# Whole-row gathers for the last four iterations of each stage of a PEER trunk

## The chip, the cores and the metric

The kernel runs on one core of a Trainium2 chip. The metric is the device time in microseconds, lower is better. Times are given as medians of several executions; a profile is one further execution, with a time of its own.

The engines that matter here are TensorE (PE, matrix products into PSUM), VectorE (DVE), ScalarE (ACT), GpSimd (POOL, which issues the gathers), and the core's 16 DMA engines.

## The reference

A decoder trunk of four layers works on 256 tokens of width 1024. Each layer has a token mixer (HGRN2, FoX attention, Mamba-2, HGRN2), and behind it a PEER block. PEER is what the change touches. For each token and each of 8 heads it scores two sets of 128 sub-keys, takes the 16 best of the 16 x 16 sums, and so gets 16 expert numbers out of 16384 with softmax gates. Then

```python
u = jnp.take(u_tab, idx, axis=0)
v = jnp.take(v_tab, idx, axis=0)
act = jax.nn.gelu(jnp.einsum('md,mhkd->mhk', xb, u), approximate=False) * gates
return jnp.einsum('mhk,mhkd->md', act, v)
```

So each token reads 128 rows of `u_tab` and up to 128 rows of `v_tab`, 4 KB each in float32, for every layer. Where the GELU is exactly zero, the V row adds nothing and needs no reading. The arguments of the GELU are spread wide by the inputs' scale, so that this happens.

## The kernel before

**Stages and iterations.** There are eight stages: four layers by two blocks of 128 tokens. Stage s runs 64 iterations, one for each pair (head, q), and each iteration handles two experts for all 128 tokens. Its 256 rows are laid out as two halves: half g holds tokens 64 g to 64 g + 63, with the first expert of the pair on partitions 0 to 63 and the second on partitions 64 to 127. In this text k is the number of an iteration within its stage (`i % 64` in the code), from 0 to 63; numbers from 64 up belong to the next stage.

**Buffers.** U and V lie side by side in one table `uv`, a row of 8 KB holding [U|V]. Eight buffers `GB` (L197), each 128 x 2048 floats (1.05 MB), take the gathered rows: iteration i uses `GB[2i % 8]` for half 0 and `GB[(2i+1) % 8]` for half 1. A pair's buffers are thus used again four iterations later.

**Gathers.** POOL issues all of them, in the order of the program. `fetch` (L1268) gathers U or whole rows; for half 1 always whole [U|V] rows, for half 0 the U half only, except in the first eight iterations of the program (`WHOLE`). In this text these are W(k) for half 1, and U(k) for half 0. `fetches(n)` (L1277) runs at the head of each iteration and sends U and W up to three iterations ahead. `second` (L1283) gathers the V rows of half 0, V(k), once the GELU of half 0 is known: two DVE instructions (L1296, L1297) add a large number to the row's index where the GELU is zero, and the gather's bounds check then leaves the row out. In the last two iterations of a stage (`early`, L1265) V(k) is gathered one iteration sooner, from the plain index (L1292, L1293), with no row left out.

**One iteration.** `fetches`, `dot` of half 0 and of half 1 (L1301: DVE multiplies U by the tokens' activations XR and sums, ACT takes the GELU), `second`, then `spread` (L1315): ACT multiplies by the gates and makes a 128 x 64 matrix of them for each half (`dg`), and PE multiplies these with the V rows (L1335) and adds into two PSUM banks. Half 1 is summed in its own iteration. Half 0 is summed `LAG` = 2 iterations later, since V(k) comes in late; in the last two iterations of a stage and in the first eight of the program it is summed in its own iteration. Behind this stand three steps of routing on DVE (which experts the next heads take) and a slot of side work: the mixer and the query projection for stage s + 1, whose weights come by SP's DMA queue.

**End of a stage.** After iteration 62 all remaining side work is done, and `repeated()` (L1246, L1463) puts 64 small products on PE's queue: they lay out the next stage's activations. ACT and DVE copy them from PSUM to XR (L1442 and L1453 on ACT, L1454 on DVE) during iteration 63, each after the `dot` that reads the old XR. The `dot` of the next stage's first iteration stands behind these copies. Up to three pairs of the next stage have been gathered ahead by then.

The engines take their instructions in program order. A gather into a buffer waits (on POOL, in order) until those who read the buffer before are done; everything that POOL has to issue behind it waits too.

Of the kernel before, what the change touches and what calls it, by code (L numbers as in the profile page):

```python
# [10 lines left out]
F32 = mybir.dt.float32  # L11
# [5 lines left out]
OP = mybir.AluOpType  # L17
AX = mybir.AxisListType

P = 128  # L20
T = 256
D = 1024
DC = D // P
DEPTH = 4
# [4 lines left out]
NQ = TOPK // 2  # L29
NGB = 8  # L30
NRAW = 3
LAG = 2
WHOLE = 8
FAR = 1048576.0
STAGES = 2 * DEPTH

# [132 lines left out]
def trunk(ctx: ExitStack, tc: tile.TileContext, d: dict, out: bass.AP):  # L169
    nc = tc.nc  # L170
# [3 lines left out]
    wk2 = ctx.enter_context(tc.tile_pool(name="wk2", bufs=2))  # L174
# [22 lines left out]
    GB = [at_["gb"][:, i * 2 * D:(i + 1) * 2 * D] for i in range(NGB)]  # L197
# [12 lines left out]
    vec = Vector()  # L210
# [79 lines left out]
    for l in range(DEPTH):  # L290
        nm = ("hg%d" % (l // 3), "fox", "ssm", "hg%d" % (l // 3))[l]
        n = UNITS[KIND[l] if KIND[l] != "ssd" else "ssm"]
# [8 lines left out]
    for u in range(28, len(stream)):  # L301
        t, l, i, where = places[u]
# [864 lines left out]
    def route(s, hh):  # L1167

        l = s // 2
        sv = wk2.tile([P, 2, TOPK], F32, name="sv")  # L1170
        si = wk2.tile([P, 2, TOPK], U32, name="si", bufs=1)
        sf = wk2.tile([P, 2, TOPK], F32, name="sf", bufs=1)
        ts = wk2.tile([P, TOPK], F32, name="ts")
        ti = wk2.tile([P, TOPK], U32, name="ti", bufs=1)
        ab = wk2.tile([P, 2, TOPK], U32, name="ab", bufs=1)
        af = wk2.tile([P, 2, TOPK], F32, name="af", bufs=1)
        cs = wk2.tile([P, TOPK * TOPK], F32, name="cs", bufs=1)
        eq = cs.bitcast(BF16).rearrange("p (c k j) -> p c k j", c=2, k=TOPK)
        cs = cs.rearrange("p (a b) -> p a b", a=TOPK)
        ix = wk2.tile([P, 2, NQ], I32, name="ix", bufs=4)  # L1180
        gs = wk2.tile([P, 2, 2, NQ], F32, name="gs", bufs=4)
        gt = wk2.tile([P, 4], F32, name="gt")
        ig = wk2.tile([P, 2, TOPK], F32, name="ig")
        yield from top16([(sv[:, c], si[:, c], SS[:, hh, c]) for c in range(2)])
        vec.tensor_copy(sf, si)
        tm(cs, sv[:, 0].unsqueeze(2).to_broadcast([P, TOPK, TOPK]),
           sv[:, 1][:, None, :].to_broadcast([P, TOPK, TOPK]), op=OP.add)
        yield
        yield from top16([(ts, ti, cs.rearrange("p a b -> p (a b)"))])
        vec.tensor_scalar(ab[:, 0], ti, 4, None, op0=OP.logical_shift_right)  # L1190
        vec.tensor_scalar(ab[:, 1], ti, 15, None, op0=OP.bitwise_and)
        vec.tensor_copy(af, ab)
        m, z, r = (gt[:, i:i + 1] for i in range(3))
        vec.tensor_scalar(m, ts[:, 0:1], -1.0, None, op0=OP.mult)
        act(ig[:, 1], ts, AF.Exp, bias=m, accum_out=z)
        yield
        eqv = eq.rearrange("p c k j -> p (c k) j")
        tm(eqv, C("iota")[:, None, :].to_broadcast([P, 2 * TOPK, TOPK]),
           af.rearrange("p c k -> p (c k)").unsqueeze(2).to_broadcast([P, 2 * TOPK, TOPK]), op=OP.is_equal)
        yield  # L1200
        tm(eq, eq, sf.unsqueeze(2).to_broadcast([P, 2, TOPK, TOPK]), op=OP.mult)
        yield
        vec.tensor_reduce(af.rearrange("p c k -> p (c k)"), eqv, axis=AX.X, op=OP.add)
        vec.tensor_scalar(sf[:, 0], af[:, 0], float(P), float(l * P * P), op0=OP.mult, op1=OP.add)
        tm(ig[:, 0], sf[:, 0], af[:, 1], op=OP.add)
        yield
        igv = ig.rearrange("p c (q j) -> p c q j", j=2)
        places = [(slice(j * 64, j * 64 + 64), g, slice(g * 64, g * 64 + 64), j) for j in range(2) for g in range(2)]

        def scaled():  # L1210
            vec.reciprocal(r, z)
            vec.tensor_scalar(ig[:, 1], ig[:, 1], r, None, op0=OP.mult)

        if (s, hh) == (0, 0):

            for o, g, i, j in places:
                vec.tensor_copy(ix[o, g], igv[i, 0, :, j])
            scaled()
            for o, g, i, j in places:
                vec.tensor_copy(gs[o, g, 1], igv[i, 1, :, j])  # L1220
        else:
            scaled()
            yield
            for o, g, i, j in places:
                vec.tensor_copy(gs[o, g], igv[i, :, :, j])
            vec.tensor_copy(ix, gs[:, :, 0])
            vec.tensor_scalar(ix[:, 0], gs[:, 0, 0], 2.0, None, op0=OP.mult)
            vec.tensor_scalar(gs[:, 0, 0], gs[:, 0, 0], 2.0, 1.0, op0=OP.mult, op1=OP.add)
        got[s, hh] = ix, gs

    heads = [(s, hh) for s in range(STAGES) for hh in range(8)]
# [30 lines left out]

    parts = d["uv"].rearrange("r (k n) -> (r k) n", k=2)

    def early(i):  # L1265
        return i % 64 >= 64 - LAG

    def fetch(n):  # L1268
        i, g = divmod(n, 2)
        s, hh, q = pairs[i]  # L1270
        to, src = GB[n % NGB], d["uv"]
        if not g and i >= WHOLE:
            to, src = to[:, 0:D], parts
        nc.gpsimd.indirect_dma_start(to, None, src,  # L1274
                                     bass.IndirectOffsetOnAxis(ap=got[s, hh][0][:, g, q:q + 1], axis=0))

    def fetches(n):  # L1277

        while sent[0] < 2 * len(pairs) and sent[0] < 2 * n + NGB and pairs[sent[0] // 2][:2] in got:
            fetch(sent[0])  # L1280
            sent[0] += 1

    def second(i):  # L1283

        if i < WHOLE or i >= len(pairs):
            return
        s, hh, q = pairs[i]
        iv = wk2.tile([P, 1], I32, name="iv", bufs=4)
        row = got[s, hh][1][:, 0, 0, q:q + 1]
        to = GB[2 * i % NGB][:, D:2 * D]  # L1290
        if early(i):
            nc.vector.tensor_copy(iv, row)  # L1292
            nc.gpsimd.indirect_dma_start(to, None, parts, bass.IndirectOffsetOnAxis(ap=iv, axis=0))  # L1293
        else:
            far = wk2.tile([P, 1], F32, name="far", bufs=2)
            nc.vector.tensor_scalar(far, acts[i][:, 1, 0:1], 0.0, FAR, op0=OP.is_equal, op1=OP.mult)  # L1296
            nc.vector.tensor_tensor(iv, far, row, op=OP.add)  # L1297
            nc.gpsimd.indirect_dma_start(to, None, parts, bass.IndirectOffsetOnAxis(ap=iv, axis=0),  # L1298
                                         bounds_check=2 * DEPTH * P * P - 1, oob_is_err=False)

    def dot(i, g):  # L1301
        if g == 0:
# [12 lines left out]
    def spread(i):  # L1315
        s, hh, q = pairs[i]
        a = acts.pop(i)
        for g in range(2):
            act(a[:, 2, g:g + 1], a[:, 1, g:g + 1], AF.Copy, scale=got[s, hh][1][:, g, 1, q:q + 1])
        for g in range(2):  # L1320
            diags[i, g] = wk2.tile([P, 64], F32, name="dg%d" % g, bufs=4 - g)
            act(diags[i, g], m64, AF.Copy, scale=a[:, 2, g:g + 1])
        if hh == 0 and q == 0:
            accs[s] = [accp.tile([P, 512], F32, name="acc") for _ in range(2)]
        if i == len(pairs) - 1:
            warm(3, bank(), cst)
        sums = [(i, 1)]
        if i < WHOLE or early(i):
            sums.append((i, 0))
        if (i - LAG, 0) in diags:  # L1330
            sums.insert(0, (i - LAG, 0))
        for e in range(2):
            for j, g in sums:
                v = GB[(2 * j + g) % NGB][:, D + e * 512:D + (e + 1) * 512]
                nc.tensor.matmul(accs[s][e][g * 64:g * 64 + 64], diags[j, g], v, start=j % 64 == 0,  # L1335
                                 stop=j % 64 == 63)
        for k in sums:
            diags.pop(k)
# [71 lines left out]
    for s in range(STAGES):  # L1410
# [23 lines left out]
        for i in range(64 * s, 64 * s + 64):  # L1434
            new, end = i % 64 == 0 and s > 0, i % 64 == 63 and s + 1 < STAGES
            fetches(i)
            if early(i + 1):
                second(i + 1)
            dot(i, 0)
            if end:  # L1440
                for o, b in x[:2]:
                    nc.scalar.copy(o, b)  # L1442
            elif new:

                products_(True)
                others()
            dot(i, 1)
            if not early(i):
                second(i)
            spread(i)  # L1450
            if end:
                (_, b), (o, c) = x[2:]
                nc.scalar.copy(x[2][0], b)  # L1453
                vec.tensor_copy(o, c)  # L1454
            route_steps(3, i // 8 + 3)
            others()
            products_()
            if i % 64 == 62 and s + 1 < STAGES:
                while not state["done"]:
                    others()  # L1460
                    products_(True)
                others()
                x = repeated()  # L1463
            if table[0] is not AF.Gelu:
                act(spare, eps, AF.Gelu)
# [20 lines left out]
```

## Time and profile before

| | us |
|---|---|
| three timed executions | 3212.19, 3215.95, 3218.97 |
| median | 3215.95 |
| the profiled execution: its own time | 3209.99 |
| the profiled execution: span of the core | 3208.2 |

| engine | busy us | share of the span |
|---|---|---|
| PE | 2506.6 | 78% |
| DVE | 2232.1 | 70% |
| POOL | 1799.3 | 56% |
| ACT | 1383.7 | 43% |

DMA moved 1271.08 MB at a mean of 396 GB/s, 1041.70 MB of them by the gathers (the queue named software_dynamic). In the rows that follow, `arena<-in_uv,ix` is a U or W gather, `arena<-in_uv,iv` a V gather; L1335 is the sum into the accumulators, L1274 the issue of U and W, L1298 and L1293 the issue of V, L207 any of the DVE helper's instructions. A row of the timeline has the start, the duration, the engine, the line and the operation, and in square brackets how long the engine was idle before it and who ended that wait. A row of the windows view has a stretch of time, its length, busy time and number of instructions of PE, PE's weight loads, DVE, ACT and POOL, then the granted PE clock (1 is full), the busy share of the DMA engines and what they moved in GB/s. The rows do not tell the iteration: it is found by counting the gathers and the sums back from the 64 products at a stage's end.

### The profile page before, as it was taken

Reading aid. Unit: us, or ns where it says so; the run is one execution under the profiler, and the core shown is the slowest. Engines: PE = TensorE matmul, PEld = TensorE weight load, DVE = VectorE, ACT = ScalarE, POOL = GpSimd, SP = SyncE. Lnnn points to the kernel's source line nnn. Section 1 sums busy time; section 2 is a strip of 40 time slices with the busy share of each in tenths; the row PEclk is TensorE's granted clock in tenths of the full one; section 3 lists DMA queues with packets and bytes.
Section 4 is the critical chain, followed back from the end, with each engine's and each line's share of the span. In section 5 each row is a group of like instructions: output and inputs, shape, how many; then the busy total and the mean of one; then the engine's idle time right before and its main releaser. Section 6 shows DMA issues by size and latency. Waiting matters only on the chain.

```text
span 3208.2 us, 33399 instructions
## 1 busy us (share of the span) xinstructions
PE 2506.6 (78%) x8610; PEld 989.7 (31%) x8610; DVE 2232.1 (70%) x6702; ACT 1383.7 (43%) x4407; POOL 1799.3 (56%) x1536
## 2 busy tenths in 40 slices
PE   9888786876787866999778898778876887875565
PEld 4423232232233322334223343323322333321111
DVE  2587757775776856888567887567766777668774
ACT  3363324363344523577234673245433544333332
POOL 0265656555765646554565545566655655567774
PEclk9998898988898988999888999889888899987767
DMA  7899999999999999999999999999999999999998
GB/s 295 342 411 415 409 402 377 415 412 416 409 368 416 400 413 385 394 416 405 417 405 355 408 415 404 408 361 413 415 415 402 365 416 416 412 370 402 408 413 329
DMA packets 252623, 1271.08 MB, mean 396 GB/s; under 512 B 35902, under 2 KB 36286, under 8 KB 158608
## 3 DMA queue, kind: packets, MB, share of 16 engines
q0 software_dynamic: 220032, 1041.70, 81.2%
q1 hardware_dynamic: 32400, 227.24, 17.2%
q8 instruction: 70, 1.15, 0.1%
q14 instruction: 121, 0.99, 0.1%
HBM read 1299.92 MB, written 1.05 MB: 406 GB/s over the span
## 4 chain that ended last, share of the span: by engine, by line
DMA 37%; issue 15%; DVE 14%; PE 12%; POOL 11%; ACT 5%; POOLq 0%; DVEq 0%; ACTq 0%
DMA arena<-in_uv,iv 26%; DMA arena<-in_uv,ix 10%; DVE arena L207 8%; POOL arena L1274 8%; PE acc L1335 6%; PE pj L242 4%; POOL arena L1298 3%; ACT L220 2%; PE ps L242 2%; DVE cs L207 1%; ACT arena L220 1%; DVE gs L207 1%; DVE iv L1297 1%; DVE af L207 1%; DVE si L207 1%
## 5 line engine op out<-in xcount | busy, mean ns | idle before, releaser
L1335 PE MATMUL acc<-arena,dg 128*64 128x512 f32 x4096 | 1318.9, 720 | 675.6 <-DMA arena<-in_uv,iv 597.5
L1274 POOL DMA_INDIRECT arena<-in_uv,ix x1024 | 1212.6, 1184 | 1067.5 <-PE acc L1335 640.0
L207 DVE SCALAR_TENSOR_TENSOR arena<-arena 128x1024 f32<-128x1024 f32 (+3 forms) x1282 | 1299.0, 1045 | 382.0 <-DMA arena<-in_uv,ix 380.3
L1335 PEld LDWEIGHTS acc<-arena,dg 128*64 128x64 f32 x4096 | 364.5, 154 | 1441.0 <-DMA arena<-in_uv,iv 861.0
L1298 POOL DMA_INDIRECT arena<-in_uv,iv x488 | 563.4, 1155 | 311.5 <-DVE iv L1297 93.3
L220 ACT ACTIVATE dots<-dots 128x1 f32<-128x1 f32 x1024 | 190.4, 199 | 1165.5 <-DVE arena L207 1164.6
L242 PE MATMUL pj<-raw,arena 128*128 128x512 f32 (+1 forms) x1368 | 642.4, 613 | 1.0 <-ACT arena L657 0.7
L220 ACT ACT_TABLE_LOAD x325 | 417.0, 1283 | 5.4 <-DVE arena L207 0.8
L242 PEld LDWEIGHTS pj<-raw,arena 128*128 128x128 f32 x1368 | 253.3, 196 | 398.5 <-issue 376.9
L220 ACT ACTIVATE dg<-m,dots 128x64 f32<-128x64 f32 x1024 | 292.6, 333 | 0.9 <-PE acc L1335 0.8
L242 PE MATMUL pj<-arena 128*128 128x512 f32 x568 | 265.7, 613 | 2.0 <-DMA arena<-in_hg 1.6
L220 ACT ACTIVATE dots<-dots,gs 128x1 f32<-128x1 f32 x1024 | 239.8, 281 | 0.0
L1296 DVE TENSOR_SCALAR far<-dots 128x1 f32<-128x1 f32 x488 | 72.9, 149 | 221.2 <-ACT dots L220 221.1
L242 PEld LDWEIGHTS pj<-arena 128*128 128x128 f32 x568 | 105.5, 195 | 161.0 <-issue 150.8
L242 PE MATMUL ps<-arena 128*128 128x128 f32 (+3 forms) x992 | 131.4, 289 | 1.1 <-ACT arena L1128 0.9
L242 PEld LDWEIGHTS ps<-arena 128*128 128x128 f32 (+2 forms) x992 | 101.8, 168 | 68.7 <-issue 40.9
L246 PE MATMUL ps<-fst,arena 128*128 128x128 f32 x568 | 91.7, 289 | 9.7 <-DVE arena L207 6.5
L220 ACT ACTIVATE arena<-arena 128x512 f32<-128x512 f32 (+3 forms) x132 | 67.7, 554 | 64.3 <-DVE arena L207 62.3
L246 PEld LDWEIGHTS ps<-fst,arena 128*128 128x128 f32 x568 | 67.3, 146 | 88.9 <-issue 49.5
L1297 DVE TENSOR_TENSOR iv<-far,gs 128x1 int32<-128x1 f32 x488 | 77.7, 159 | 16.8
L207 DVE DVE_READ_ACCUMULATOR arena<-arena 128x1 f32 x1024 | 83.3, 81 | 0.0
L1115 ACT COPY arena<-ps 128x512 f32<-128x512 f32 x31 | 18.1, 583 | 134.1 <-PE ps L242 134.1
(123 smaller groups left out, 1521.5 us busy)
## 6 DMA issues: line engine op xcount, KB each, us to landing
raw<-in_hg SPq DMA_DIRECT2D x57, 1024.0 KB, 9.1
raw<-in_ssm SPq DMA_DIRECT2D x56, 1024.0 KB, 8.9
raw<-in_wq SPq DMA_DIRECT2D x32, 1024.0 KB, 9.0
raw<-in_fox SPq DMA_DIRECT2D x24, 1024.0 KB, 9.1
arena<-in_wq SPq DMA_DIRECT2D x17, 1024.0 KB, 15.7
arena<-in_uv,ix POOLq DMA_INDIRECT x1024, 10.3
arena<-in_hg SPq DMA_DIRECT2D x15, 1024.0 KB, 14.4
arena<-in_uv,iv POOLq DMA_INDIRECT x504, 10.1
```

The source lines that it names most:

```text
L207: return getattr(nc.vector, name)(o, *a, **k)
L220: nc.scalar.activation(o, i, f, **k)
L242: nc.tensor.matmul(o, w, m, start=start, stop=stop)
L246: nc.tensor.transpose(o, i, ident)
L1115: nc.scalar.copy(SS[:, 2 * g:2 * g + 2], b.rearrange("p (h c k) -> p h c k", h=2, c=2))
L1274: nc.gpsimd.indirect_dma_start(to, None, src, bass.IndirectOffsetOnAxis(ap=got[s, hh][0][:, g, q:q + 1], axis=0))
L1296: nc.vector.tensor_scalar(far, acts[i][:, 1, 0:1], 0.0, FAR, op0=OP.is_equal, op1=OP.mult)
L1297: nc.vector.tensor_tensor(iv, far, row, op=OP.add)
L1298: nc.gpsimd.indirect_dma_start(to, None, parts, bass.IndirectOffsetOnAxis(ap=iv, axis=0), bounds_check=2 * DEPTH * P * P - 1, oob_is_err=F ...
L1335: nc.tensor.matmul(accs[s][e][g * 64:g * 64 + 64], diags[j, g], v, start=j % 64 == 0, stop=j % 64 == 63)
```

## The change

The last four iterations of a stage (`TAIL`, k = 60 to 63) gather whole [U|V] rows for half 0 as well; this text calls such a gather w(k). They need no `second`, and are summed in their own iteration. The four iterations ahead of them (k = 56 to 59) keep U and V apart, but V(k) is summed one iteration later in place of two, so that its buffer is free in time for w(k + 4). The plain form of `second`, with its early issue, is gone. w(k) is issued at the head of iteration k - 2, ahead of W(k + 1), where U(k) was issued at the head of iteration k - 3. In the last head of a stage the last four index columns stay plain row numbers.

```diff
-LAG = 2
 WHOLE = 8
+TAIL = 4
...
             vec.tensor_copy(ix, gs[:, :, 0])
-            vec.tensor_scalar(ix[:, 0], gs[:, 0, 0], 2.0, None, op0=OP.mult)
-            vec.tensor_scalar(gs[:, 0, 0], gs[:, 0, 0], 2.0, 1.0, op0=OP.mult, op1=OP.add)
+            a = NQ - TAIL if hh == 7 else NQ
+            vec.tensor_scalar(ix[:, 0, 0:a], gs[:, 0, 0, 0:a], 2.0, None, op0=OP.mult)
+            vec.tensor_scalar(gs[:, 0, 0, 0:a], gs[:, 0, 0, 0:a], 2.0, 1.0, op0=OP.mult, op1=OP.add)
...
-    def early(i):
-        return i % 64 >= 64 - LAG
+    def lag(i):
+        if i < WHOLE or i % 64 >= 64 - TAIL:
+            return 0
+        return 1 if i % 64 >= 64 - 2 * TAIL else 2
...
-        if not g and i >= WHOLE:
+        if not g and lag(i):
             to, src = to[:, 0:D], parts
...
+        def last(i):
+            return WHOLE <= i < len(pairs) and not lag(i)
+
+        if last(n + 2):
+            fetch(2 * n + 4)
         while sent[0] < 2 * len(pairs) and sent[0] < 2 * n + NGB and pairs[sent[0] // 2][:2] in got:
-            fetch(sent[0])
+            if sent[0] % 2 or not last(sent[0] // 2):
+                fetch(sent[0])
             sent[0] += 1
...
     def second(i):
-        if i < WHOLE or i >= len(pairs):
+        if not lag(i):
             return
...
-        if early(i):
-            nc.vector.tensor_copy(iv, row)
-            nc.gpsimd.indirect_dma_start(to, None, parts, bass.IndirectOffsetOnAxis(ap=iv, axis=0))
-        else:
...
-        sums = [(i, 1)]
-        if i < WHOLE or early(i):
-            sums.append((i, 0))
-        if (i - LAG, 0) in diags:
-            sums.insert(0, (i - LAG, 0))
+        sums = [(i, 1)] + [(j, 0) for j in (i, i - 2, i - 1) if (j, 0) in diags and j + lag(j) == i]
...
             fetches(i)
-            if early(i + 1):
-                second(i + 1)
             dot(i, 0)
...
-            if not early(i):
-                second(i)
+            second(i)
             spread(i)
```

More of the change, by code (lines that the diff above doesn't have):

```diff
@@ L1288, in second @@
         iv = wk2.tile([P, 1], I32, name="iv", bufs=4)
-        row = got[s, hh][1][:, 0, 0, q:q + 1]
-        to = GB[2 * i % NGB][:, D:2 * D]
-        if early(i):
-            nc.vector.tensor_copy(iv, row)
-            nc.gpsimd.indirect_dma_start(to, None, parts, bass.IndirectOffsetOnAxis(ap=iv, axis=0))
-        else:
[L1295 to L1299, printed above, removed]
+        far = wk2.tile([P, 1], F32, name="far", bufs=2)
+        nc.vector.tensor_scalar(far, acts[i][:, 1, 0:1], 0.0, FAR, op0=OP.is_equal, op1=OP.mult)
+        nc.vector.tensor_tensor(iv, far, got[s, hh][1][:, 0, 0, q:q + 1], op=OP.add)
+        nc.gpsimd.indirect_dma_start(GB[2 * i % NGB][:, D:2 * D], None, parts,
+                                     bass.IndirectOffsetOnAxis(ap=iv, axis=0),
+                                     bounds_check=2 * DEPTH * P * P - 1, oob_is_err=False)
     def dot(i, g):
```

## The prediction

> **What bounds the kernel now.** First the page: its head, the slices of DMA, the gathers' queue and the chain that ended last.
>
> ```profile
> span 3208.2 us, 33399 instructions
> DMA  7899999999999999999999999999999999999998
> GB/s 295 342 411 415 409 402 377 415 412 416 409 368 416 400 413 385 394 416 405 417 405 355 408 415 404 408 361 413 415 415 402 365 416 416 412 370 402 408 413 329
> q0 software_dynamic: 220032, 1041.70, 81.2%
> DMA 37%; issue 15%; DVE 14%; PE 12%; POOL 11%; ACT 5%; POOLq 0%; DVEq 0%; ACTq 0%
> ```
>
> No engine is as full as the DMA engines, and they run near 415 GB/s but for dips: the start, the end, and seven slices spaced like the ends of the stages. So I looked for the products that lay out the next activations (64 small ones at each stage's end) and took a window of 30 us around each of the seven; the first and the last are shown, the others moved 289, 310, 306, 286 and 313 GB/s. Then one of them, at 2114 us, in short windows.
>
> ```profile
> 510.00:540.00 30.00, 20.06 (x106) 8.38 (x108) 19.49 (x62) 14.35 (x44) 14.80 (x14) 0.84 0.87 314
> ...
> 2868.00:2898.00 30.00, 21.05 (x105) 8.60 (x107) 19.87 (x61) 10.78 (x38) 14.39 (x14) 0.84 0.81 289
> ```
>
> ```profile
> 2085.00:2105.00 20.00, 11.46 (x36) 3.37 (x32) 15.08 (x43) 7.58 (x27) 16.34 (x13) 0.84 1.02 415
> ...
> 2115.00:2120.00 5.00, 5.00 (x67) 3.97 (x64) 1.71 (x2) 2.58 (x8) 0.32 (x1) 1.00 0.81 308
> 2120.00:2125.00 5.00, 1.99 (x6) 0.47 (x4) 3.98 (x18) 1.25 (x6) 1.87 (x2) 1.00 0.45 134
> 2125.00:2130.00 5.00, 4.37 (x10) 0.94 (x8) 4.93 (x16) 2.48 (x10) 3.26 (x4) 0.66 0.84 265
> 2130.00:2135.00 5.00, 2.51 (x8) 0.47 (x6) 4.90 (x15) 3.61 (x9) 4.08 (x4) 1.00 0.79 243
> ```
>
> The mean of the seven is 301 GB/s; against 415 in the saturated stretch ahead, a boundary loses 30 x (1 - 301/415) = 8.2 us of transfer time, 58 us in all. Only this can be won. Why it is lost stands in the timeline of the same boundary: PE first (sums, and the 64 products), then POOL, then the copies.
>
> ```profile
> 2079.55 3.75 PE L1335 MATMUL acc<-arena,dg 128*64 128x512 f32 x8 [1.20 <-DMA arena<-in_uv,iv]
> 2084.42 3.48 PE L1335 MATMUL acc<-arena,dg 128*64 128x512 f32 x8 [1.12 <-DMA arena<-in_uv,iv]
> 2089.37 2.00 PE L1335 MATMUL acc<-arena,dg 128*64 128x512 f32 x8 [1.47 <-DMA arena<-in_uv,iv]
> 2094.21 3.70 PE L1335 MATMUL acc<-arena,dg 128*64 128x512 f32 x8 [2.84 <-DMA arena<-in_uv,iv]
> ...
> 2109.18 4.53 PE L1335 MATMUL acc<-arena,dg 128*64 128x512 f32 x7 [3.28 <-DMA arena<-in_uv,iv]
> ...
> 2114.36 3.88 PE L242 MATMUL ps<-fst,arena 128*64 128x128 f32 x62
> 2118.07 3.60 PE L1335 MATMUL acc<-arena,dg 128*64 128x512 f32 x12
> ...
> 2137.86 3.04 PE L1335 MATMUL acc<-arena,dg 128*64 128x512 f32 x8 [3.27 <-DMA arena<-in_uv,iv]
> ```
>
> ```profile
> 2078.62 1.56 POOL L1274 DMA_INDIRECT arena<-in_uv,ix  x1 [2.45 <-PE acc L1335]
> 2080.49 1.00 POOL L1298 DMA_INDIRECT arena<-in_uv,iv  x1 [0.30 <-issue]
> ...
> 2085.58 1.00 POOL L1298 DMA_INDIRECT arena<-in_uv,iv  x1 [0.30 <-issue]
> ...
> 2099.46 1.87 POOL L1293 DMA_INDIRECT arena<-in_uv,iv  x1 [0.30 <-DVE iv L1292]
> ...
> 2113.15 0.94 POOL L1274 DMA_INDIRECT arena<-in_uv,ix  x1 [4.38 <-remote]
> ...
> 2121.12 0.94 POOL L1274 DMA_INDIRECT arena<-in_uv,ix  x1 [5.80 <-PE acc L1335]
> ```
>
> ```profile
> 2118.29 0.69 DVE L207 COPY arena<-ps 128x512 f32<-128x512 f32 x1 [14.05 <-PE ps L242]
> 2118.90 1.22 DVE L207 SCALAR_TENSOR_TENSOR arena<-arena 128x1024 f32<-128x1024 f32 x1
> ```
>
> Counted back from the 64 products, the sums are those of k = 57 (2079.55, released by V(55)), 58 (V(56) landed at 2084.42), 59 (V(57), 2089.37), 60 (V(58), 2094.21); V(62), issued at 2099.46, lands at 2109.18 and releases the rest of sum 62. Only behind this come the products, the copies, and at 2118.90 the next stage's first dot. DVE has stood 14.05 us, POOL's W(66) waited for sum 62 and W(67) for sum 63 (2121.12): the DMA runs dry at about 2120.
>
> The landings obey one rule, which carries the sum below: the gathers move one behind another at 415 GB/s, so that U takes 0.524 MB / 415 = 1.26 us, W 2.53. V: of 1041.70 MB, 809.5 are U and whole rows (512 W of 1.0486 MB, 8 whole and 504 U of half 0); of the 264.2 MB of V, 8.4 are gathered without a test, and the 223.8 left of 255.9 are 87.5%, so V takes 1.10 us. Check: V(57) at 2089.37 + U + W + V = 2094.26; the row says 2094.21.
>
> **The change, part by part.** I follow the same boundary.
>
> *k = 57, the shorter lag.* Head 57 sends W(60) at 2078.62 and V(57) at 2080.49 as before, but no U(60). V(56) still lands at 2084.42; V(57) at 2084.42 + 2.53 + 1.10 = 2088.05. Sum 57 now needs V(56) and ends at about 2084.42 + 3.48 = 2087.90, where it ended at 2083.3. Behind it on PE are only the next sums. But w(60) needs the V half that sum 57 reads, so POOL stands until 2088.2, and behind it W(61) and V(58), which was issued at 2085.58. Nothing is left to transfer from 2088.05. How long from issue to the first byte? The shortest gathers give a bound:
>
> ```profile
> DMA to landing us min/median/max: 4.1/10.2/29.7
> DMA to landing us min/median/max: 5.1/10.3/30.3
> ```
>
> (V and U/W.) 5.1 less a W's 2.53 is 2.6 us; if the 5.1 was a U, 3.8; V's 4.1 - 1.1 gives 3.0. I take 2.6: transfer starts at 2090.8 and **the first drain costs 2.75 us**. If the sum takes the 2.00 of the row at 2089.37, it is 1.3; with 3.8 to the first byte 4.0.
>
> The Trainium skill (DMA: Bandwidth & Descriptors, Anatomy of one DMA) puts a gather at a fixed 2.0 us plus its bytes at 436 GB/s: 4.4 us for a W. No gather of U or W here landed so soon; the 5.1 is against it. By the Trainium skill the drain would be about 0.7 us shorter, and the time 5 us lower.
>
> *k = 58 to 61.* w(60), W(61), V(58) land at 2093.3, 2095.8, 2096.9. Sum 58 ends at about 2091.5 (V(57) is there), then w(61), W(62), V(59): 2099.4, 2102.0, 2103.1. Sum 59 waits for V(58) and ends by 2099 to 2100.6; w(62) and W(63) follow: 2105.6, 2108.1, without a gap. Sum 60 waits for V(59) at 2103.1 and ends between 2105.1 and 2106.9; w(63) issues 0.3 later, and first bytes at 2108.0 to 2109.8 stand against 2108.1: a **second drain of 0 to 1.7, taken as 0.9**. w(63) lands at 2111.5; U(64) to W(66) follow to 2122.9, as dots and sums 60 to 62 have freed their buffers.
>
> *k = 62 and the restart.* No V is waited for now. w(62) lands at 2105.6; two dots and ACT's part stand between it and sum 62:
>
> ```profile
> L207 DVE SCALAR_TENSOR_TENSOR arena<-arena 128x1024 f32<-128x1024 f32 x8 | 9.5, 1219 | 1.0 <-DMA arena<-in_uv,ix 1.0
> ...
> L220 ACT ACTIVATE dg<-m,dots 128x64 f32<-128x64 f32 x8 | 2.3, 332 | 0.0
> L220 ACT ACTIVATE dots<-dots,gs 128x1 f32<-128x1 f32 x7 | 1.7, 279 | 0.0
> L220 ACT ACTIVATE dots<-dots 128x1 f32<-128x1 f32 x7 | 1.4, 201 | 10.4 <-DVE arena L207 10.3
> ```
>
> Twice 1.22 and 0.20 + 2 x (0.28 + 0.33) make 3.9: 2109.5. Sum 62 ends at 2111.5, the products 3.9 later at 2115.4, the copy at 2116.2: the first dot is 2.7 us ahead of 2118.90. W(67), freed by sum 63, comes at 2117.7 in place of 2121.12, while the queue is busy until 2122.9. It stays busy: W(67) lands at 2126.7, V(64) at 2127.8, and at 4.89 us an iteration V(65) at 2132.7 where the row of 2137.86 stood. That is 5.1 us for this boundary, of a loss that was 30 x (1 - 286/415) = 9.3.
>
> *What is removed, and more bytes.* Four V gathers a stage leave POOL and six small instructions leave DVE:
>
> ```profile
> L1297 DVE TENSOR_TENSOR iv<-far,gs 128x1 int32<-128x1 f32 x488 | 77.7, 159 | 16.8
> ```
>
> POOL and DVE stand waiting for buffers and landings there, which hides this work, so I put it at nothing; uncovered it would be worth 4 x (1.00 + 0.30) = 5.2 us a stage on POOL and 6 x 0.16 = 1.0 on DVE. V(60) and V(61) are read without a test: 2 x 12.5% of 0.524 MB is **0.3 us a stage**. The routing's instructions keep their number.
>
> *After the drain.* From 2125 to 2135 the engines were 79 to 84% busy at 243 to 265 GB/s: with few gathers queued each moves less. A stretch of 5 us like that costs 5 x (1 - 265/415) = 1.8, part of it in the drain already. I add **1.0** (0 to 1.8).
>
> *The last stage* has no boundary to win, and w(63) needs dots after landing, where V(63) was only summed.
>
> ```profile
> 3162.98 1.86 POOL L1274 DMA_INDIRECT arena<-in_uv,ix  x1 [0.60 <-PE acc L1335]
> ...
> 3169.14 3.49 PE L1335 MATMUL acc<-arena,dg 128*64 128x512 f32 x8 [3.04 <-DMA arena<-in_uv,iv]
> ...
> 3187.18 0.94 POOL L1293 DMA_INDIRECT arena<-in_uv,iv  x1 [3.15 <-DVE arena L207]
> ...
> 3197.27 3.65 PE L1335 MATMUL acc<-arena,dg 128*64 128x512 f32 x12
> ```
>
> V(56) lands at 3169.14 there, V(57) at 3172.8. The same steps: w(60) first moves at 3175.5; V(58) lands at 3181.6, V(59) at 3187.8, w(63) between 3195.3 and 3196.7 (the queue is short now, so both drains are met); with 3.9 us of dots and ACT and 2.4 of sum it ends between 3201.6 and 3203.0, against 3197.27 + 3.65 = 3200.9. I take **+1.5**, range 0 to +4.
>
> *Sum.* A boundary wins 8.2 - 2.75 - 0.9 - 0.3 - 1.0 = 3.3; seven win 23, less 1.5 at the end: **-21.5**. The profiled execution (span 3208.2, own time 3209.99) is 6 us under the median; the edit doesn't touch that difference, so the median goes from 3215.95 to **3194.5**. Bounds: at best 8.2 - 1.3 - 0.3 = 6.6 a boundary, -46; at worst 8.2 - 4.0 - 1.7 - 0.3 - 1.8 = 0.4, and +4 at the end: +1. Alone, the forecast's own range is 3180 to 3206.
>
> **Rivals.**
>
> *Slower: every iteration of the short lag drains the queue.* The place is POOL at the heads 58 to 61, each held by a sum that waits for a V issued only one iteration earlier. If the queue is empty each time, four drains at 2.75 and the bytes cost 11.3 against 8.2: +3.1 a boundary, +23 with the end, **3239**. It decides once drains exceed 7.9 us a boundary. For it: POOL has just the 3.6 us of W(60) and V(57) behind V(56). Against: from the second on, five or six transfers are queued when the sum ends, 4 to 6 us by my table.
>
> *No change: the gain is given back within the stage.* Side work fills PE ahead of a stage's end, and DMA dips there:
>
> ```profile
> 2059.00:2074.00 15.00, 10.83 (x45) 4.06 (x43) 10.52 (x38) 7.09 (x24) 9.26 (x9) 0.99 0.99 382
> ```
>
> If that stretch ended when it did before, what the boundary won would be waited off, and only one boundary's 3.3 us and the end would remain: about -2, **3214**. Against: side work is paced by iterations, and most slices between show over 400 GB/s, so an earlier start should carry through.
>
> *Larger: nearly the whole dip goes.* If sum 57 takes 2.00 us, and the second drain and the thin stretch don't come: 6.6 a boundary, **3170**. Against: three of four sums above last 3.5 or more.
>
> **Chances.** Forecast 0.55, larger 0.12, no change 0.14, slower 0.19. A difference under 0.2% (6.4 us) can't be told here from no change. Faster is then 0.67, within 0.14, slower 0.19. The range 3168 to 3222 takes in both bounds and leaves out most of the slower case.
>
> **What would show it.** Right: the seven windows at 350 GB/s or more, a gap of 1 to 4 us in the transfers some 28 us ahead of the 64 products, DVE's wait ahead of the copy short, sum 62 released by ACT and no longer by a V gather. Wrong: POOL idle 3 us or more at each of the heads 58 to 61, or windows unchanged because the next dots start no earlier; the last sum more than 5 us later would put the end at a higher price than mine.

## The result, and the profile after

| | before | changed |
|---|---|---|
| median of four timed executions, us | 3214.57 | 3234.85 |
| lowest to highest, us | 3212.19 to 3218.97 | 3230.56 to 3240.12 |
| span of the profiled execution, us | 3208.2 | 3228.8 |

The changed kernel takes 1.0062 times as long (95% interval 1.0043 to 1.0081): 20.3 us slower, where 21.5 us faster was forecast. One execution of a later experiment, e3_laststage (3468.29 us at a granted clock of 0.72, where the others had 0.88 to 0.92), is left out of every comparison. The page's head of the changed kernel: the dips have not gone.

```profile
span 3228.8 us, 33237 instructions
DMA  7899999999999998999999999999999999999997
GB/s 294 348 412 415 414 402 365 416 414 416 360 412 407 395 416 347 414 415 394 417 374 391 395 416 405 399 368 415 416 416 371 391 416 415 414 359 415 414 411 286
q0 software_dynamic: 215424, 1042.81, 80.5%
```

The windows of 30 us around the 64 products, the first and the last of seven, laid as in the prediction (the products start at 514.94 and 2887.51 here); and the 26 us ahead of each of these windows, first and last again.

```profile
510.00:540.00 30.00, 19.14 (x106) 7.25 (x106) 24.71 (x72) 16.31 (x53) 20.30 (x19) 0.89 1.01 406
...
2883.00:2913.00 30.00, 19.20 (x105) 7.29 (x106) 23.34 (x69) 13.06 (x49) 19.16 (x19) 0.83 1.01 410
```

```profile
484.00:510.00 26.00, 16.08 (x44) 4.54 (x44) 11.14 (x34) 6.84 (x22) 10.00 (x10) 0.74 0.72 271
...
2857.00:2883.00 26.00, 13.93 (x40) 3.90 (x36) 11.30 (x26) 6.50 (x21) 11.55 (x11) 0.81 0.76 278
```

The same 26 us before the change, at two of the boundaries:

```profile
484.00:510.00 26.00, 14.30 (x36) 3.86 (x36) 18.39 (x51) 8.21 (x30) 17.69 (x15) 0.68 1.02 414
2084.00:2110.00 26.00, 13.76 (x38) 4.03 (x40) 16.04 (x47) 8.07 (x29) 20.19 (x16) 0.76 1.02 414
```

This is the whole result in two views. The seven windows around the products moved 406, 403, 397, 404, 405, 410 and 410 GB/s, a mean of 405 where it was 301: their loss fell from 8.2 to 30 x (1 - 405/415) = 0.7 us. The 26 us ahead moved 271, 265, 266, 313, 284, 277 and 278, a mean of 279, where the seven of before, laid in the same way, had 391 to 417, a mean of 410 (a loss of 0.3): the loss there is now 26 x (1 - 279/415) = 8.5 us. **The dip has moved ahead by some 25 us, and is no smaller.**

What makes it is seen at the boundary that the prediction followed; everything there comes 11.6 us later than before, since earlier boundaries have cost time. POOL's, PE's and DVE's timeline of the changed kernel:

```profile
2085.22 1.00 POOL L1301 DMA_INDIRECT arena<-in_uv,iv  x1 [0.30 <-DVE si L207]
2089.20 0.94 POOL L1277 DMA_INDIRECT arena<-in_uv,ix  x1 [2.97 <-PE acc L1335]
2090.44 1.38 POOL L1301 DMA_INDIRECT arena<-in_uv,iv  x1 [0.30 <-issue]
2100.11 0.94 POOL L1277 DMA_INDIRECT arena<-in_uv,ix  x1 [8.29 <-PE acc L1335]
2101.36 0.94 POOL L1277 DMA_INDIRECT arena<-in_uv,ix  x1 [0.31 <-issue]
...
2114.59 1.71 POOL L1277 DMA_INDIRECT arena<-in_uv,ix  x1 [7.06 <-PE acc L1335]
2116.61 0.94 POOL L1277 DMA_INDIRECT arena<-in_uv,ix  x1 [0.30 <-issue]
2120.41 0.94 POOL L1277 DMA_INDIRECT arena<-in_uv,ix  x1 [2.86 <-PE acc L1335]
```

```profile
2095.36 6.20 PE L1335 MATMUL acc<-arena,dg 128*64 128x512 f32 x18 [3.94 <-DMA arena<-in_uv,iv]
2110.65 5.38 PE L1335 MATMUL acc<-arena,dg 128*64 128x512 f32 x10 [9.09 <-DMA arena<-in_uv,iv]
2116.86 4.51 PE L1335 MATMUL acc<-arena,dg 128*64 128x512 f32 x16 [0.84 <-DMA arena<-in_uv,iv]
2124.10 1.94 PE L1335 MATMUL acc<-arena,dg 128*64 128x512 f32 x8 [2.73 <-ACT dg L220]
2125.87 3.66 PE L242 MATMUL ps<-fst,arena 128*64 128x128 f32 x64
```

```profile
2105.43 1.23 DVE L207 SCALAR_TENSOR_TENSOR arena<-arena 128x1024 f32<-128x1024 f32 x1 [7.70 <-DMA arena<-in_uv,ix]
...
2113.12 1.22 DVE L207 SCALAR_TENSOR_TENSOR arena<-arena 128x1024 f32<-128x1024 f32 x1 [2.84 <-DMA arena<-in_uv,ix]
...
2120.59 1.22 DVE L207 SCALAR_TENSOR_TENSOR arena<-arena 128x1024 f32<-128x1024 f32 x1 [3.04 <-DMA arena<-in_uv,ix]
...
2127.95 1.23 DVE L207 SCALAR_TENSOR_TENSOR arena<-arena 128x1024 f32<-128x1024 f32 x1 [4.99 <-DMA arena<-in_uv,ix]
...
2131.05 1.22 DVE L207 SCALAR_TENSOR_TENSOR arena<-arena 128x1024 f32<-128x1024 f32 x1
```

V(56) is issued at 2085.22, lands at 2095.36 and lets PE go on with sum 57. W(60) is issued at 2089.20 and V(57) at 2090.44; then POOL stands 8.29 us and issues w(60) at 2100.11, 4.75 us after V(56) landed. Only W(60) and V(57) lay behind V(56), 2.53 + 1.10 us of transfer. The dot on w(60) starts at 2105.43; the dots of w(61), w(62) and w(63) follow at 2113.12, 2120.59 and 2127.95, some 7.5 us apart, where the two whole gathers of an iteration take 2 x 2.53 (and a V, in the first two of these stretches, 1.10). POOL is held a second time before w(62) (7.06 us, by sum 59, which waited for V(58) until 2110.65) and a third before w(63) (2.86). Sum 62 is released by ACT (2124.10). The next stage's first dot is at 2131.05, that is 2119.45 on the clock of before: 0.6 us behind the old 2118.90.

The short windows there: from 2095 to 2105 the DMA engines are busy 46% and 67% of the time, from 2120 to 2125 they are busy 94% and still move no more than 326 GB/s.

```profile
2095.00:2100.00 5.00, 4.64 (x13) 1.61 (x15) 2.60 (x11) 1.80 (x7) 0.00 (x0) 0.66 0.46 189
2100.00:2105.00 5.00, 1.56 (x7) 0.38 (x3) 0.00 (x0) 2.66 (x5) 3.82 (x4) 1.00 0.67 224
...
2115.00:2120.00 5.00, 4.16 (x16) 1.21 (x15) 2.33 (x11) 1.05 (x5) 2.24 (x2) 0.89 0.73 256
2120.00:2125.00 5.00, 2.27 (x8) 0.54 (x8) 2.38 (x4) 1.25 (x6) 3.68 (x4) 1.00 0.94 326
```

To compare kernels, one sum over the DMA packets of each trace serves below: for every us the moved bytes' shortfall against 415 GB/s, added up **ahead** (from the dot of k = 55 to the dot of k = 62) and **behind** (from there to the dot of k = 8 of the next stage, or to the end).

```
lost transfer time, us        ahead/stage  behind/stage   last stage: ahead, behind
                              (mean of 7)  (mean of 7)
before                            1.0          8.6            0.2    16.0
changed                           9.5          1.2           10.5    14.1
e2_oldorder                       9.0          2.3
e3_laststage                      9.8          2.2            0.1    16.9
e4_lag                            5.9          9.7            4.7    15.4
e5_tail2                          7.3          8.5            7.8    15.2
e10_earlyv                        2.4          3.0            2.1    14.1
e11_earlyv2                       6.0          2.4            6.8    13.5
e6_products                       1.2          5.7
e8_vfirst                         1.0          4.6
e9_both                           1.1          2.1
```

From before to changed: 7 x (9.5 - 1.0) = +60 ahead, 7 x (1.2 - 8.6) = -52 behind, +10.3 - 1.9 in the last stage, together +16; 1.1 MB more at 415 GB/s are 2.7. That is 19 of the 20.6 us.

### The profile page after: what moved, and what is told of

It is laid out like the page before. It is cut to its first block, busy times and chain, and to the rows that moved or that the text cites. A ratio compares the mean times of both kernels' runs of the same rounds, so it can differ in the third digit from the quotient of the medians.

```text
span 3228.8 us, 33237 instructions
## 1 busy us (share of the span) xinstructions
PE 2527.0 (78%) x8610; PEld 948.1 (29%) x8610; DVE 2230.5 (69%) x6654; ACT 1386.5 (43%) x4407; POOL 1759.9 (55%) x1504
## 3 DMA queue, kind: packets, MB, share of 16 engines
q0 software_dynamic: 215424, 1042.81, 80.5%
## 5 line engine op out<-in xcount | busy, mean ns | idle before, releaser
L1335 PE MATMUL acc<-arena,dg 128*64 128x512 f32 x4096 | 1356.2, 697 | 676.9 <-DMA arena<-in_uv,iv 473.4
L1277 POOL DMA_INDIRECT arena<-in_uv,ix x1024 | 1196.1, 1168 | 1125.5 <-PE acc L1335 651.4
L1335 PEld LDWEIGHTS acc<-arena,dg 128*64 128x64 f32 x4096 | 332.9, 150 | 1515.4 <-DMA arena<-in_uv,iv 703.1
L220 ACT ACTIVATE dg<-m,dots 128x64 f32<-128x64 f32 x1024 | 292.7, 333 | 20.3 <-PE acc L1335 20.2
```

The source lines that it names most:

```text
L220: nc.scalar.activation(o, i, f, **k)
L1277: nc.gpsimd.indirect_dma_start(to, None, src, bass.IndirectOffsetOnAxis(ap=got[s, hh][0][:, g, q:q + 1], axis=0))
```

## The experiments

The theory after the result: the shorter lag holds POOL, and with it every gather, until after the queue has emptied. The expectations call it A. The rivals: the order in which a sum takes its halves, which the diff also turns round in all iterations (B); the last stage alone (C); the whole rows themselves (more bytes, later issue), the shorter lag being hidden (D).

**e2_oldorder**: the changed kernel, with the lagging half summed first again, as before the change.

```diff
-        sums = [(i, 1)] + [(j, 0) for j in (i, i - 2, i - 1) if (j, 0) in diags and j + lag(j) == i]
+        sums = [(j, 0) for j in (i - 2, i - 1) if (j, 0) in diags and j + lag(j) == i] + [(i, 1)]
+        sums += [(i, 0)] if not lag(i) else []
```

> The changed kernel with the order of the sums of before: the lagging half 0 first, then half 1, in every iteration. Theory A (the drains): the time goes into two refills of the empty DMA queue ahead of every stage's end; the order of the sums is not it, so this stays with the changed kernel, 3230 to 3240 us. Rival B (the order of the sums slows the steady iterations): about 20 us come back, 3212 to 3220 us.

Measured: 3235.39, ratio to before 1.0072 (1.0053 to 1.0090), against 1.0062 for the change as it is. The order of the sums is worth nothing that can be told; that rival falls.

**e3_laststage**: the changed kernel, with the last stage left as it was before (lag 2, V(62) and V(63) gathered early).

```diff
-        if i < WHOLE or i % 64 >= 64 - TAIL:
+        if i < WHOLE or i % 64 >= 64 - TAIL and i < 448 or i >= 510:
             return 0
-        return 1 if i % 64 >= 64 - 2 * TAIL else 2
+        return 1 if i % 64 >= 64 - 2 * TAIL and i < 448 else 2
...
+            if early(i + 1):
+                second(i + 1)
             dot(i, 0)
```

> The changed kernel in the first seven stages, the last stage as before (U and V apart, V summed two iterations later, the plain early gather in its last two iterations). Theory A: the last stage has no next stage's gathers to put behind, so there the drains win nothing; its 7 us come back and the seven boundaries stay: 3225 to 3231 us, and in the trace the last stage from its first to its last dot takes what it took before. Rival C (the end costs no more than I forecast, 1.5 us): 3232 to 3236 us.

Measured: 3229.0 (median of four), ratio 1.0041 (1.0025 to 1.0057). This interval overlaps that of the changed kernel (1.0043 to 1.0081), so the times alone do not settle it; the trace does. In the last stage the loss ahead is 0.1 us again in place of 10.5. The dots of k = 55 to 63 there drift by 0.5 us against before; in the changed kernel it is 16.8, and at the end 7.5 of that are left (13.1 us behind at k = 8 of this stage, 20.6 at the end). So the last stage's price is 5 to 7 us, and most of the 20 comes from the seven boundaries.

**e4_lag**: the kernel before, with nothing changed but the lag: V(56) to V(59) are summed one iteration later. No whole rows.

```diff
-        if (i - LAG, 0) in diags:
-            sums.insert(0, (i - LAG, 0))
+        for j in (i - 1, i - 2):
+            if (j, 0) in diags and j + (1 if 56 <= j % 64 < 60 else LAG) == i:
+                sums.insert(0, (j, 0))
```

> The kernel before, with only one thing of the change: V(56) to V(59) are summed one iteration later in place of two; no whole rows, the last two iterations as before. Theory A: sum 57 waits for V(56) and W(61) behind it, with only U(61) sent in between, so the queue drains about 4 us a stage ahead of the old loss: 8 x 3 to 5 us, 3235 to 3255 us. Rival D (the shorter lag is hidden by the 10 us that are queued, and the whole rows or their place in the order cost the time): 3212 to 3220 us.

Measured: 3265.41, ratio 1.0164 (1.0147 to 1.0181), some 51 us or 6.4 a stage, worse than expected. This is the decisive run: the shorter lag alone costs more than the whole change does. POOL's timeline and the window beside it, at the same stage's end:

```profile
2117.79 0.94 POOL L1274 DMA_INDIRECT arena<-in_uv,ix  x1 [9.29 <-PE acc L1336]
```

```profile
2115.00:2120.00 5.00, 4.43 (x14) 1.14 (x10) 1.84 (x4) 3.76 (x9) 1.90 (x2) 0.80 0.53 168
```

A hold of 9.29 us, and 168 GB/s in the stretch around its end. The loss ahead rises from 1.0 to 5.9 a stage, while the old loss behind stays (9.7).

**e5_tail2**: the changed kernel with whole rows in the last two iterations alone; V(58) to V(61) have the shorter lag.

```diff
-TAIL = 4
+TAIL = 2
...
-        return 1 if i % 64 >= 64 - 2 * TAIL else 2
+        return 1 if i % 64 >= 64 - 3 * TAIL else 2
```

> The changed kernel with whole rows for half 0 in the last two iterations of a stage alone (k = 62 and 63); V(58) to V(61) are summed one iteration later. Theory A: w(62) and W(63) wait for one sum that is late, w(63) for the next one, which is ready: one refill of about 5 us a stage in place of two of 5.3 and 3.5, so that a boundary wins 2 to 3 us over before and the end loses 3 to 5: 3198 to 3212 us. Rival D (whole rows cost what they cost wherever they stand): half of what four cost, about 3225 us.

Measured: 3260.79, ratio 1.0156 (1.0130 to 1.0183). The expectation missed by 49 us and more. Two things were overlooked in it: V(61) at lag 1 is again what sum 62 and the products wait for, so that the old loss behind stays at 8.5; and the one long hold of the queue that is left costs 7.3 ahead by itself. POOL's timeline, PE's, and three windows:

```profile
2118.36 0.94 POOL L1277 DMA_INDIRECT arena<-in_uv,ix  x1 [9.41 <-PE acc L1335]
```

```profile
2135.60 4.53 PE L1335 MATMUL acc<-arena,dg 128*64 128x512 f32 x7 [3.10 <-DMA arena<-in_uv,iv]
```

```profile
2115.00:2120.00 5.00, 4.80 (x14) 1.53 (x10) 0.08 (x1) 0.59 (x2) 1.34 (x2) 0.72 0.03 9
...
2145.00:2150.00 5.00, 1.70 (x8) 0.29 (x4) 4.97 (x15) 1.25 (x7) 1.31 (x2) 1.00 0.29 70
```

From 2115 to 2120 the queue is all but dry (9 GB/s), at 2145 a second time (70 GB/s), behind a sum released by a V gather, as before the change.

**e10_earlyv**: the changed kernel, with V(56) to V(59) issued one iteration sooner, from the plain index (so that no row is left out of these).

```diff
+        if lag(i) == 1:
+            nc.vector.tensor_copy(iv, got[s, hh][1][:, 0, 0, q:q + 1])
+            nc.gpsimd.indirect_dma_start(GB[2 * i % NGB][:, D:2 * D], None, parts,
+                                         bass.IndirectOffsetOnAxis(ap=iv, axis=0))
+            return
...
             fetches(i)
+            if lag(i + 1) == 1:
+                second(i + 1)
             dot(i, 0)
...
-            second(i)
+            if lag(i) != 1:
+                second(i)
```

> The changed kernel, with V(56) to V(59) gathered one iteration sooner, at the head of k - 1 and from the plain index, no row left out; their lag of one iteration and the whole rows of 60 to 63 stay. This takes away what the late sums wait for. Theory A (the late sums hold POOL and drain the DMA queue ahead of the stage's end): the loss ahead of dot 62, 9.5 us a stage in the changed kernel against 1.0 before, falls to 1 to 3, and the one behind it stays at about 1; with 5 us of more bytes in all the time is 3175 to 3190 us, under both kernels. Rival D (the whole rows, or POOL's order w(k) ahead of W(k+1), drain the queue by themselves): no better than 3225 us.

Measured: 3187.72, ratio 0.9919 (0.9898 to 0.9940): 27 us under before and 47 under the changed kernel. POOL's timeline, and the windows from there:

```profile
2074.51 0.94 POOL L1277 DMA_INDIRECT arena<-in_uv,ix  x1 [6.83 <-PE acc L1340]
```

```profile
2070.00:2075.00 5.00, 5.00 (x17) 1.45 (x14) 4.59 (x13) 2.19 (x11) 0.49 (x1) 0.78 1.00 414
2075.00:2080.00 5.00, 3.18 (x12) 0.79 (x9) 0.43 (x4) 3.29 (x6) 3.78 (x5) 1.00 0.90 317
```

POOL is still held 6.83 us, but DMA moves 414 GB/s to the end of the hold, since U(59), W(59), V(57), W(60) and V(58) lie by then behind V(55), the last gather that sum 57 waits for here: 8.5 us of transfers and more. The loss ahead is 2.4 us a stage, not 9.5. So it is the lateness of V behind the held sum that costs, not the whole rows.

**e11_earlyv2**: the same for V(56) and V(57) alone.

```diff
+    def plain(i):
+        return lag(i) == 1 and i % 64 < 58
...
-        if lag(i) == 1:
+        if plain(i):
```

> The changed kernel, with V(56) and V(57) alone gathered one iteration sooner from the plain index; V(58) and V(59) as in the changed kernel. Theory A with two drains of their own, of about 5.5 us (sum 57 waits for V(56)) and 3.5 us (sums 59 and 60 wait for V(58) and V(59)) a stage: the first goes and the second stays, 8 x 5 us less 3 us for more bytes, 3194 to 3205 us, and a loss ahead of dot 62 of 4 to 5 us a stage. Rival G (one late stretch: what is not waited for at sum 57 is waited for at sum 59): 3220 us or more, with a loss of 8 or more.

Measured: 3216.84 over ten executions, ratio 1.0014 (0.9996 to 1.0033): some 15 us under the changed kernel by the ratios, and between the two expectations. The loss ahead is 6.0 us a stage, between them too. POOL's timeline:

```profile
2089.21 0.94 POOL L1280 DMA_INDIRECT arena<-in_uv,ix  x1 [9.45 <-PE acc L1343]
...
2102.68 1.92 POOL L1280 DMA_INDIRECT arena<-in_uv,ix  x1 [5.82 <-PE acc L1343]
```

w(60) is held as long as ever (9.45), w(62) 5.82. The gathers of V(56) and V(55), sum 57 on PE, and the window from the end of its wait to w(60)'s issue, here and (last row) in the changed kernel:

```profile
2070.55 0.94 POOL L1303 DMA_INDIRECT arena<-in_uv,iv  x1 [0.30 <-issue]
2071.79 1.00 POOL L1309 DMA_INDIRECT arena<-in_uv,iv  x1 [0.31 <-issue]
```

```profile
2082.97 7.68 PE L1343 MATMUL acc<-arena,dg 128*64 128x512 f32 x20 [1.15 <-DMA arena<-in_uv,iv]
```

```profile
2082.97:2089.21 6.24, 6.24 (x16) 2.00 (x17) 4.38 (x14) 1.66 (x9) 0.00 (x0) 0.62 0.91 379
2095.36:2100.11 4.75, 4.75 (x15) 1.71 (x17) 2.24 (x11) 1.78 (x6) 0.00 (x0) 0.64 0.41 169
```

Sum 57 takes three halves: its own half 1, V(55) at a lag of two and V(56) at a lag of one, two products each. V(56) now stands in the queue ahead of V(55), while the sum takes V(55) first, so what it waits for is V(55). Against the dots this wait ends 3.3 us sooner than the one for V(56) did in the changed kernel, but w(60) goes out only 1.8 sooner: five of the sum's six products are still to come after the wait, where it was four, at nearly the same granted clock (0.62 and 0.64). So the price of each drain by itself is not cleanly measured by this run. That the two are worth about half each can be said, no more.

The last three runs try the kernel before from the other side: leave the lag alone, and end the old loss by order.

**e6_products**: before, with what is left of the side work and the 64 products put ahead of sum 62.

```diff
             dot(i, 1)
             if not early(i):
                 second(i)
+            if i % 64 == 62 and s + 1 < STAGES:
+                while not state["done"]:
+                    others()
+                    products_(True)
+                others()
+                x = repeated()
             spread(i)
...
-            if i % 64 == 62 and s + 1 < STAGES:
-                while not state["done"]:
-                    others()
-                    products_(True)
-                others()
-                x = repeated()
```

> The kernel before, with the end of the side work and the 64 products put ahead of sum 62 on PE's queue. Theory E (the old loss at the boundary starts with the products standing behind V(62) on PE): the copies and the next stage's first dot come 8 to 12 us sooner, V(64) some 3 us sooner since W(67) ahead of it still waits for sum 63; 2 to 4 us a boundary, 3186 to 3200 us. Rival F (the buffers, not DVE's restart, set the loss): 3210 to 3218 us.

**e8_vfirst**: before, with the next stage's gathers of the heads 61 and 62 issued behind the V gathers of these iterations.

```diff
-            fetches(i)
+            ahead = i % 64 in (61, 62)
+            if not ahead:
+                fetches(i)
...
                 second(i)
+            if ahead:
+                fetches(i)
             spread(i)
```

> The kernel before, with the next stage's gathers of iterations 61 and 62 issued behind V(62), V(61) and V(63) instead of ahead. V(62) then lands 3.8 us sooner (U(64) and W(64) were ahead of it), sum 62 and the products with it. Theory E: the first dot and W(66) come 3 to 4 us sooner, 2 to 4 us a boundary: 3186 to 3200 us. Rival F: 3210 to 3218 us.

**e9_both**: e6_products and e8_vfirst together.

```diff
                 second(i)
+            if ahead:
+                fetches(i)
+            if i % 64 == 62 and s + 1 < STAGES:
+                while not state["done"]:
...
             spread(i)
```

> The kernel before with both: the products ahead of sum 62, and the next stage's gathers of iterations 61 and 62 behind the V gathers. Theory E: W(66) and W(67) are freed by sums 62 and 63, which now come 4 us sooner and are no longer behind the products; 4 to 6 us a boundary, 3172 to 3190 us. Rival F: 3205 us or more.

Measured: e6_products 3196.98, ratio 0.9948 (0.9927 to 0.9968); e8_vfirst 3188.84, 0.9920 (0.9899 to 0.9941); e9_both **3169.26**, 0.9869 (0.9847 to 0.9890), the last a little under its expected range. The wins of the two, 17.8 and 26.0 us, add up to 43.8; both together win 45.5. The first copy of the products on DVE in e6_products, in e8_vfirst and in e9_both, in this order:

```profile
2104.60 0.69 DVE L207 COPY arena<-ps 128x512 f32<-128x512 f32 x1 [5.50 <-remote]
```

```profile
2109.82 0.69 DVE L207 COPY arena<-ps 128x512 f32<-128x512 f32 x1 [9.38 <-PE ps L242]
```

```profile
2082.76 0.69 DVE L207 COPY arena<-ps 128x512 f32<-128x512 f32 x1 [1.76 <-PE ps L242]
```

The wait ahead of it was 14.05 us before; it is 5.50, 9.38 and 1.76, and the loss behind goes from 8.6 to 5.7, 4.6 and 2.1 with the loss ahead untouched (1.0 to 1.2). e9_both beats before by 45 us and the changed kernel by 66. The old loss was thus the late V(62) in front of the products, as the prediction had it, and could be won without whole rows.

## Why the prediction was wrong

**What bounds the kernel, and the old loss: right.** That the boundary's loss is DMA waiting for sum 62's V, and that whole rows end it, holds: the forecast said windows of 350 GB/s or more, a gap some 28 us ahead of the products, sum 62 released by ACT. All three came (405; no packet starts from 2099.0 to 2101.5, 24 to 27 us ahead of the products at 2125.87; ACT at 2124.10). Of the 8.2 us that could be won, 7.5 were, by the same windows. Bytes were right too: 1.1 MB more, 1042.81 against 1041.70.

**The price of the drains: mis-sized, above all "I add 1.0 (0 to 1.8)" for the time after them; this is the step that failed.** The forecast had "the first drain costs 2.75 us", "a second drain of 0 to 1.7, taken as 0.9", and this 1.0. The mechanism was named, at its place, POOL held by sum 57 at the issue of w(60). V(57) landed 3.7 us behind V(56), forecast 3.63. From there:

- V(58) landed 11.56 us behind V(57). Without a gap W, W and V take 2.53 + 2.53 + 1.10 = 6.16; so the first drain, with the slow transfers behind it, cost **5.4**. w(60) went out 4.75 us behind V(56)'s landing (forecast 3.78), its dot began 5.32 after its issue (forecast 5.13), and then W(61), issued 1.25 us behind it, landed about 3.9 us later in place of 2.53. Each was a little late, and the last was not in the sum at all but as part of the 1.0.
- The second drain was forecast at the head of k = 60's sum. It comes one sum sooner: sum 59 waited for V(58), late by the first drain, and w(62) was issued 3.94 us behind its landing (2110.65 to 2114.59), when W(62) and V(59) were all that was queued. From then w(62), W(63) and w(63) landed 3.74, 3.71 and 3.65 us apart in place of 2.53: **3.5** us, forecast 0.9. The prediction's "five or six transfers are queued when the sum ends, 4 to 6 us by my table" counted transfers as if the queue had been full again after the first drain; its own table has 2.5 to 4.1 us left at the end of sum 59 (2099 to 2100.6, against V(59) at 2103.1).

Together 8.9 us where 2.75 + 0.9 + 1.0 = 4.65 stood. By the shortfall's table the mean over the seven is 8.5.

The packets of the trace split this. At this boundary no packet is under way for 3.2 us (2098.6 to 2101.8) and again for 0.6 us (2116.4 to 2117.0); over the seven boundaries the means are 3.5 and 0.6. The dry time is thus 4.0 us a stage, near the forecast 2.75 + 0.9 = 3.65, in part by luck: w(60) was issued 1.0 us later than forecast, and its first packet came 1.7 us after the issue, where 2.6 was taken. What remains, 8.5 - 4.0 = 4.5 us a stage, is transfers that move too slowly behind the dry time, and for these the sum had 1.0, at most 1.8.

Dry time and slow transfers together, 8.5 us in place of 4.65, take 3.85 x 7 = 27 us from the forecast; the smaller win behind the products (7.4 in the table) takes 0.8 x 7 = 5.6.

By an estimate from the Trainium skill (DMA: Bandwidth & Descriptors, Anatomy of one DMA), w(60) would have landed 4.4 us after its issue. The trace differs: its dot starts 5.32 us after the issue, and the 5.13 of the prediction was nearly right; the Trainium skill's figure would have put the sum further off.

**"+1.5" for the last stage: mis-sized.** The steps were the right ones (both drains are met, w(63) needs its dots), but the drains are the larger ones, so the last sum ends at 3220.7 by the row below, against 3200.9 before, of which 13.1 us are drift from earlier stages: about 7.

```profile
3218.74 1.94 PE L1335 MATMUL acc<-arena,dg 128*64 128x512 f32 x8 [1.75 <-ACT dg L220]
```

The sum then reads -21.5 + 27 + 5.6 + 5.5 = +17, against +20.6 in span. From k = 8 to 55, which the forecast left unchanged, the changed kernel loses another 0.4 us a stage in the mean of one execution of each (from 1.5 gained to 3.4 lost); this was not looked into.

**The rivals.** "Slower: every iteration of the short lag drains the queue" gave 3239, and 3234.85 came. Its point of decision, 7.9 us of drains a boundary, was passed (8.9, slow transfers included), so it is the case that came nearest, but not by its mechanism: not four drains at 2.75 but two, at 5.4 and 3.5, over half of which is not dry time; w(61) was issued without a hold. "No change" is refuted in its reason: the loss is not side work between the stages but lies within 26 us of the products. "Larger" falls with the drains.

**Overlooked.** The diff turns the order of the sums round in every iteration; the prediction did not mention it. It turned out to be worth nothing (e2_oldorder), so that the forecast was lucky there. And e4_lag would have been the sum to make first: what does the shorter lag cost alone? 6.4 us a stage, against the 2.75 + 0.9 that was put on it.

## What to carry to other kernels

When one engine issues all transfers in order and is to stand for a consumer, count what is queued behind the transfer that the consumer waits for: it must last longer than consumer, issue and first landing together. Here 3.6 us of transfers stood against 4.75 + 5.32 - 2.53 = 7.5 us, and the queue ran dry; with V issued one iteration sooner the hold stayed and most of its cost went (2.4 us of loss ahead, where it was 9.5). The dry time is not the whole price either: 4.0 us of it a stage came with 4.5 us of slow transfers. A buffer freed sooner by a consumer that has to wait is no gain, and a stall at a stage's end may be had more cheaply by putting its order right (e9_both) than by removing what it waits for.

## What the hardware showed unexpectedly

**The queue that had run empty did not restart at full rate.** In the trace's packets, 8 KB rows take a median of 0.312 us on their engine. In the first us after the queue had been empty they took 0.66 on average (2101 to 2102), and with only two or three gathers queued 0.57 (2117 to 2118) and 0.54 (2120 to 2121); before the change, after the old dry spell, 0.98 (2122 to 2123). The engines are then counted busy, 94% of the time at 2120 to 2125, and move 326 GB/s, and gathers land 3.7 us apart in place of 2.53. In the four windows shown the engines are idle for 5 x (0.54 + 0.33 + 0.27 + 0.06) = 6.0 us, and the shortfall against 415 GB/s is 5 x (4 - 995/415) = 8.0. What makes these packets slow was not tried.
